# Weights read as every second column of a slab, in the main products of a decoder step

## The chip, the cores and the metric

The kernel runs on one core of one Trainium2 chip. The metric is device time in microseconds of one execution. Before the change it is 1634.39 us (median of three runs, 1634.28 to 1634.63). The profile shows a further execution, instruction by instruction.

## The reference

One step of a decoder layer, for 256 prompt rows and 8 x 4 sample rows with the same weights, so T = 288 rows in all, D_MODEL = 2048 and D_FF = 8192:

```
h = rms_norm(x);  proj = h @ w_in            # 2048 x 10752: conv, attention, memory, gates
y_conv = silu(layer_norm(conv31(glu))) @ w_conv_out
y_sb   = stick_breaking(q, k, v) @ w_sb_out  # 8 heads
y_mem  = softmax_attention(qm, mem) @ w_mem_out   # 4 heads, 256 memory tokens
x = x + (gates * (y_conv, y_sb, y_mem)) summed @ w_o
x = x + square(relu(rms_norm(x) @ w_up)) @ w_down
```

All values are float32. Besides the rows y the new keys, values and convolution rows are returned. Nearly all the arithmetic is in the products of the 288 rows with w_in, w_o, w_up and w_down.

## The kernel before, in words

**Layout.** Activations lie transposed: features on the 128 partitions, the 288 rows along the free side. A product is computed in output tiles of 128 features by 288 rows, one PSUM bank each (pool `pm`). The weight block of 128 x 128 is the operand that TensorE holds (the first operand of `nc.tensor.matmul(ps, w, a)`, line 488), the activation tile of 128 x 288 is the one that it streams, "moving".

**Slabs.** The host lays all weights out in one array `wall` of 504 slabs, each 128 partitions x 1024 floats (`_layout`, from line 1481). From slab 16 on a slab is eight blocks of 128 columns; two slabs make one output tile over 2048 input features. Slabs 0 to 15 belong to the memory keys and values, where `mem_products` (line 541) takes the roles the other way round: 512 slab columns are moving, and the activations are held.

**High and low parts.** To keep float32 accuracy with the faster float32r format, each operand is split: a high part, rounded by a cast, and a low part, the remainder. A weight slab comes by DMA on the sync queue into one of 4 raw tiles `wr` (`load_slab`, line 283), ScalarE casts it into `wh` (line 305), VectorE subtracts into `wl` (line 316). Activations have tiles for `h` and `l` likewise. A block then needs three matmuls: high x high, high x low, low x high. `products` (line 494) lists the 24 matmuls of a slab, first 16 with `wh`, then 8 with `wl`, and gives them to `chunk` (486) six at a time. `conv_products` (550) does the same for the first eight slabs of w_in, in its own order; `main_tile` (509) and `branch_products` (1387) call `products` for everything else. With 488 slabs these are 11,712 matmuls.

**Places in memory.** The `wh` and `wl` tiles are 1088 floats long, and from slab 16 on the weights start `SHIFT` = 5 floats into the tile (`shifted`, line 286). Activation tiles `a` are 320 floats long with the data `AHEAD` = 4 floats in (`Acts`, 325); in the MLP the tiles of the pools `k4` and `s` hold them, 36 floats in (`HOME`, line 1248), three to a tile of 1024 with a distance of 320. For the memory part the activations start 32 floats in, and slabs 0 to 15 at 0.

**Order.** A planner (`Order`, line 75) runs while the program is built. Each piece of work is a generator that asks for an engine and says how long it will take (`MM` = 0.131 us for a matmul of 288 columns) and which flags and buffers it waits for. The planner fixes the order on every engine; on the chip each engine goes through its own list and waits on semaphores. TensorE's list is `main` (1413): memory keys and values, convolution inputs, heads, the three branches with their gates, w_o, then four times 16 tiles of w_up and 16 tiles of w_down. The attention of prompt and samples is mixed in between, up to about 436 us.

Of the kernel before, what the change touches and what calls it, by code (L numbers as in the profile page):

```python
# [14 lines left out]
P = 128  # L15
D_MODEL = 2048
KT = D_MODEL // P
# [19 lines left out]
N_SLABS = 504  # L37
# [37 lines left out]
class Order:  # L75
# [15 lines left out]
    def add(self, gen, rank, at=None):  # L91
        job = Job(gen, rank, self.now.ready if at is None and self.now else at or 0.0)
        self.jobs.append(job)
        was, self.now = self.now, job
        self.step(job)
        self.now = was
# [10 lines left out]
    def give(self, pool, n=1):  # L107
        self.pools[pool] += [self.now.ready] * n
# [57 lines left out]
def pe(us, *flags, **take):  # L166
    return Ask("PE", us, flags, **take)
# [16 lines left out]
def tile_decoder_step(ctx: ExitStack, tc: tile.TileContext, xT, memT, wall, cvec, kmat, ptab,  # L184
# [27 lines left out]
    def bank(p):  # L212
        return tl(p, [P, 512])
# [107 lines left out]
    def start_slab(s):  # L321
        at_slab[:] = [s, order.now.ready]
# [10 lines left out]
    hm, hx = [None] * KT, [None] * KT  # L333
# [149 lines left out]
        done(rm_done)  # L483


    def chunk(ps, todo, first, last):
        for i, (w, a) in enumerate(todo):
            nc.tensor.matmul(ps, w, a, start=(first and i == 0), stop=(last and i == len(todo) - 1))  # L488
# [5 lines left out]
    def products(ps, uses, acts, first=True, last=True, n=T):  # L494

        s = slab_no[0] - 1
        sl = slabs[s]
        high = [(sl.h, c, a, x) for c, a in zip(uses, acts) for x in (0, 1)]
        low = [(sl.l, c, a, 0) for c, a in zip(uses, acts)]
        todo = high + low  # L500
        for i in range(0, len(todo), STEP):
            part = todo[i:i + STEP]
            yield pe(len(part) * MM, *sl.split, *{a.flag for _, _, a, _ in part})
            if i == 0 and first:
                start_slab(s)
            chunk(ps, [(w[:, c:c + P], a.l if x else a.h) for w, c, a, x in part],
                  first and i == 0, last and i + STEP >= len(todo))

    def main_tile(acts, evac, rank=1.0, n_slabs=2):
        yield pe(0.0, pm=1)  # L510
        ps = bank("pm")[:, :T]
        for i in range(n_slabs):
            slab_no[0] += 1
            yield from products(ps, FULL, acts[8 * i:8 * i + 8], i == 0, i == n_slabs - 1)
            give("w")
        add(evac(ps), rank)
# [33 lines left out]
    def conv_products(evacs):  # L550

        s0 = slab_no[0]
        slab_no[0] += KT // 2
        yield pe(0.0, pa=2)
        ps = [bank("pa")[:, :T], bank("pa")[:, :T]]
        lead = 3
        turns = [(k2, o) for k2 in range(lead) for o in (0, 1)] + [(k2, o) for k2 in range(lead) for o in (2, 3)]
        turns += [(k2, o) for k2 in range(lead, KT // 2) for o in range(4)]
        for k2, o in turns:
            s = s0 + k2  # L560
            sl = slabs[s]
            if len(ps) <= o:
                yield pe(0.0, pm=1)
                ps.append(bank("pm")[:, :T])
            todo = []
            for i in range(2):
                w = slice(i * 512 + o * P, i * 512 + (o + 1) * P)
                todo += [(sl.h, w, "h", 2 * k2 + i), (sl.h, w, "l", 2 * k2 + i)]
            for i in range(2):
                todo.append((sl.l, slice(i * 512 + o * P, i * 512 + (o + 1) * P), "h", 2 * k2 + i))  # L570
            yield pe(6 * MM, *sl.split, hx_in[2 * k2], hx_in[2 * k2 + 1])
            if o == 0:
                start_slab(s)
            chunk(ps[o], [(w[:, c], getattr(hx[k], x)) for w, c, x, k in todo], k2 == 0, k2 == KT // 2 - 1)
            if k2 == KT // 2 - 1:
                add(evacs[o](ps[o]), 1.0 + 0.01 * o)
            if o == 3:
                give("w")
        for k in range(KT):
            hx[k].flag = hx_in[k]  # L580
# [806 lines left out]
    def branch_products(br, acts):  # L1387
        for j0 in range(0, KT, 4):
            for j in range(j0, j0 + 4):
                yield from main_tile(hx, gate(br, j))  # L1390
            for j in range(j0, j0 + 4):
                if br == 1:
                    yield from main_tile(acts, branch(br, j), 1.0, 1)
                    continue
                yield pe(0.0, pm=1)
                ps = bank("pm")[:, :T]
                if j % 2 == 0:
                    slab_no[0] += 1
                yield from products(ps, [k * 2 * P + (j % 2) * P for k in range(4)], acts)
                if j % 2:  # L1400
                    give("w")
                add(branch(br, j)(ps), 1.0)
# [10 lines left out]
    def main():  # L1413
        yield from warm_up()
        yield from mem_products()
        yield from conv_products([evac_lin(0, "pa"), evac_gat(0, "pa"), evac_lin(1, "pm"), evac_gat(1, "pm")])
        for j in range(2, CT):
            yield from main_tile(hx, evac_lin(j, "pm"))
# [62 lines left out]
def _layout(inp):  # L1481
    import numpy as np

    a = {k: np.asarray(v) for k, v in inp.items()}
# [8 lines left out]
    x = np.concatenate([a["x_prompt"][0], a["x_sample"].reshape(NS, D_MODEL)], 0)  # L1493

    wall = np.empty((N_SLABS, P, SLAB), np.float32)
    at = [0]

    def put(w, j, r0=0, rows=D_MODEL):
        for half in range(rows // 1024):
            blk = w[r0 + half * 1024:r0 + (half + 1) * 1024, j * P:(j + 1) * P]  # L1500
            wall[at[0]].reshape(P, 8, P)[:] = blk.reshape(8, P, P).transpose(1, 0, 2)
            at[0] += 1
# [40 lines left out]
    for c in range(4):  # L1543
        for f in range(KT):
            put(a["w_up"][0], c * KT + f)
        for j in range(KT):
            put(a["w_down"][0], j, c * D_MODEL)
    assert at[0] == N_SLABS

    cvec = np.zeros((P, NCV), np.float32)  # L1550
    cvec[:, C_GMIX:C_GMIX + KT] = cols(a["g_mix"][0])
# [19 lines left out]
    r, c = i[:, None] % NS, np.arange(NS)[None, :]  # L1571
# [49 lines left out]
```

## Time and profile before

| what | value |
|---|---|
| median of three runs | 1634.39 us |
| span of the profiled execution, first to last instruction | 1632.5 us |
| instructions | 30962 |
| TensorE matmuls busy | 1627.7 us, 100% |
| weight loads (PEld) busy | 1610.3 us, 99% |
| VectorE busy | 992.1 us, 61% |
| ScalarE busy | 739.3 us, 45% |
| GpSimd busy | 139.1 us, 9% |
| DMA | 305.39 MB, mean 187 GB/s |

The times of runs are of a whole execution, the span is from the first instruction to the last within the profiled one; they differ by 1.9 us here. In the profile PE is TensorE's matmuls, PEld its loads of weights, which run under the matmul before them; DVE is VectorE, ACT ScalarE, POOL GpSimd, SP the sync engine with its DMA queue. A row of a group reads: line, engine, operation, tile written <- tiles read, sizes, count, then busy time, mean ns of one and idle time before. Matmuls overlap, so their mean duration is longer than the interval from one start to the next, and a busy share of 100% says only that there was no gap. Clock digits give the granted clock of TensorE in tenths, 9 standing for 90% or more. In the chain in order of time each piece has its start, its length and the number of instructions.

### The profile page before, as it was taken

What the parts mean: (1) busy time and instruction counts of PE and PEld (TensorE: products, weight loads), DVE (VectorE), ACT (ScalarE), POOL (GpSimd) and SP (SyncE); (2) the same over time, 40 slices, a digit from 0 to 9 for tenths busy, and PEclk for the clock granted to TensorE, in tenths of its full rate; (3) what the DMA queues carried; (4) which work ended last, traced back from release to release, by engine and by line L of the source; (5) the groups of instructions that cost most, each with busy time, mean ns of one, the idle gap of its engine ahead of it and who ended that gap; (6) DMA issues with size and microseconds to landing.
All of it is one profiled execution on the core that took longest, in us unless ns stands there. A gap on an engine that the chain in (4) does not pass through costs nothing.

```text
span 1632.5 us, 30962 instructions
## 1 busy us (share of the span) xinstructions
PE 1627.7 (100%) x12786; PEld 1610.3 (99%) x12786; DVE 992.1 (61%) x1471; ACT 739.3 (45%) x1070; POOL 139.1 (9%) x104
## 2 busy tenths in 40 slices
PE   9999999999999999999999999999999999999999
PEld 7999999999999999999999999999999999999999
DVE  8889888877677655565555544455445554455443
ACT  8746766644444534444443333333333333333332
POOL 0020000000000000001222200121001210022100
PEclk9999999999999999999999999999999999999999
DMA  9787465777755555546655555555555555555563
GB/s 339 217 186 251 153 209 189 248 257 252 254 166 169 163 179 167 174 153 212 191 176 168 169 168 168 169 169 174 165 173 170 168 170 169 168 168 168 180 194 99
DMA packets 107103, 305.39 MB, mean 187 GB/s; under 512 B 19922, under 2 KB 29522, under 8 KB 106962
## 3 DMA queue, kind: packets, MB, share of 16 engines
q1 hardware_dynamic: 106818, 303.39, 58.2%
q8 instruction: 100, 1.64, 0.4%
q14 instruction: 41, 0.34, 0.1%
q10 hardware_dynamic: 144, 0.02, 0.0%
HBM read 297.05 MB, written 6.32 MB: 186 GB/s over the span
## 4 chain that ended last, share of the span: by engine, by line
PE 99%; DMA 0%; SPq 0%; ACT 0%; DVE 0%; issue 0%
PE pm L488 93%; PE pm L541 3%; PE pa L488 1%; PE pl L1017 1%; PE pl L1190 0%; PE pa L854 0%; PE pa L855 0%; PE pa L853 0%; DMA wr<-in_wall 0%; PE pl L1033 0%; PE pa L827 0%; PE pa L1144 0%; PE pa L908 0%; PE pa L1141 0%; PE pa L1143 0%; PE pa L1107 0%
## 5 line engine op out<-in xcount | busy, mean ns | idle before, releaser
L305 ACT CAST wh<-wr 128x1024 fp32r<-128x1024 f32 (+1 forms) x520 | 530.3, 1022 | 648.1 <-PE pm L488 597.0
L488 PE MATMUL pm<-a,wh 128*128 128x288 f32 x5184 | 739.1, 293 | 0.0
L316 DVE TENSOR_TENSOR wl<-wr,wh 128x1024 fp32r<-128x1024 f32 (+1 forms) x520 | 617.2, 1190 | 195.2 <-ACT wh L305 190.5
L488 PEld LDWEIGHTS pm<-a,wh 128*128 128x128 f32 x5184 | 696.7, 188 | 1.3 <-issue 1.2
L488 PE MATMUL pm<-a,wl 128*128 128x288 f32 x2592 | 397.0, 292 | 0.0
L488 PEld LDWEIGHTS pm<-a,wl 128*128 128x128 f32 x2592 | 358.4, 188 | 0.0
L488 PE MATMUL pm<-k,wh 128*128 128x288 f32 x2160 | 306.7, 292 | 0.0
L488 PEld LDWEIGHTS pm<-k,wh 128*128 128x128 f32 x2160 | 290.2, 188 | 0.0
L488 PE MATMUL pm<-k,wl 128*128 128x288 f32 x1120 | 171.6, 292 | 0.0
L488 PEld LDWEIGHTS pm<-k,wl 128*128 128x128 f32 x1120 | 155.1, 188 | 0.0
L1346 POOL TENSOR_TENSOR t<-t 128x288 f32<-128x288 f32 x64 | 96.7, 1511 | 599.5 <-DVE t L1343 599.5
L1360 DVE TENSOR_TENSOR a<-a,pm 128x288 f32<-128x288 f32 x64 | 29.0, 454 | 122.4 <-PE pm L488 122.4
L1343 DVE SCALAR_TENSOR_TENSOR t<-pm,rx 128x288 f32<-128x288 f32 x64 | 29.2, 457 | 90.4 <-PE pm L488 90.4
L1349 ACT CAST k<-t 128x288 fp32r<-128x288 f32 x56 | 24.1, 433 | 115.6 <-POOL t L1346 115.6
L1262 DVE TENSOR_TENSOR t<-pm,rx 128x288 f32<-128x288 f32 x48 | 22.0, 458 | 71.5 <-PE pm L488 71.5
L488 PE MATMUL pm<-s,wh 128*128 128x288 f32 x400 | 65.1, 292 | 0.0
L719 DVE SCALAR_TENSOR_TENSOR a<-a,cv,a 128x256 f32<-128x256 f32 x120 | 57.5, 480 | 1.4
L1332 POOL TENSOR_TENSOR t<-t,t 128x288 f32<-128x288 f32 x15 | 21.6, 1441 | 419.3 <-ACT t L1329 419.3
L488 PEld LDWEIGHTS pm<-s,wh 128*128 128x128 f32 x400 | 56.6, 188 | 0.0
L1351 DVE TENSOR_TENSOR k<-t,k 128x288 fp32r<-128x288 f32 x52 | 23.8, 458 | 51.1 <-ACT k L1349 51.1
L541 PE MATMUL pm<-wh,a 128*128 128x512 f32 x128 | 34.6, 391 | 0.2 <-ACT wh L305 0.2
L488 PE MATMUL pm<-s,wl 128*128 128x288 f32 x160 | 33.8, 292 | 0.0
(212 smaller groups left out, 784.4 us busy)
## 6 DMA issues: line engine op xcount, KB each, us to landing
wr<-in_wall SPq DMA_DIRECT2D x488, 512.0 KB, 3.6
wr<-in_wall SPq DMA_DIRECT2D x32, 256.0 KB, 4.8
k<-in_kpool SPq DMA_DIRECT2D x32, 256.0 KB, 5.9
k<-in_vpool SPq DMA_DIRECT2D x32, 256.0 KB, 5.8
k<-in_mkc SPq DMA_DIRECT2D x8, 512.0 KB, 10.2
k<-in_mvc SPq DMA_DIRECT2D x8, 512.0 KB, 6.5
t<-in_xT SPq DMA_DIRECT2D x16, 144.0 KB, 3.7
out_yT<-a SPq DMA_DIRECT2D x16, 144.0 KB, 1.9
```

The source lines that it names most:

```text
L305: nc.scalar.copy(sl.h[:, c], sl.raw[:, c])
L316: nc.vector.tensor_sub(sl.l[:, c], sl.raw[:, c], sl.h[:, c].bitcast(F32))
L488: nc.tensor.matmul(ps, w, a, start=(first and i == 0), stop=(last and i == len(todo) - 1))
L541: nc.tensor.matmul(ps[m], y[:, m * P:(m + 1) * P], z[:, w], start=(k == 0 and j < 2), stop=(k == KT - 1 and j in (4, 5)))
L719: nc.vector.scalar_tensor_tensor(c[:, :NP], up[:, k:k + NP], w, c[:, :NP], op0=ALU.mult, op1=ALU.add)
L1262: nc.vector.tensor_mul(g, ps, rx)
L1332: nc.gpsimd.tensor_add(sq_sum[0], sq_sum[0], res[0])
L1343: nc.vector.scalar_tensor_tensor(r, ps, 0.0, r2, op0=ALU.max, op1=ALU.mult)
L1346: nc.gpsimd.tensor_mul(r, r, r)
L1349: nc.scalar.copy(a.h, r)
L1351: nc.vector.tensor_sub(a.l, r, a.h.bitcast(F32))
L1360: nc.vector.tensor_add(x1[j], x1[j], ps)
```

## The change

In the slabs 16 to 503 the host interleaves each pair of neighbouring 128-column blocks: column c of the first block goes to place 2c of the 256, column c of the second to 2c + 1. A weight operand is then every second float of the 256, from the first or second on. The kernel's `block` makes this view, and both callers of `chunk` use it. The moving operands, the slabs 0 to 15, the casts, the subtractions and the transfers are as they were.

```diff
+    def block(w, c):
+
+        pair = w[:, c // (2 * P) * 2 * P:(c // (2 * P) + 1) * 2 * P]
+        return pair.rearrange("p (c two) -> p two c", two=2)[:, c // P % 2]
...
-            chunk(ps, [(w[:, c:c + P], a.l if x else a.h) for w, c, a, x in part],
+            chunk(ps, [(block(w, c), a.l if x else a.h) for w, c, a, x in part],
...
-            chunk(ps[o], [(w[:, c], getattr(hx[k], x)) for w, c, x, k in todo], k2 == 0, k2 == KT // 2 - 1)
+            chunk(ps[o], [(block(w, c.start), getattr(hx[k], x)) for w, c, x, k in todo], k2 == 0, k2 == KT // 2 - 1)
...
     assert at[0] == N_SLABS
+    for s in range(KT, N_SLABS):
+        v = wall[s].reshape(P, 4, P, 2)
+        v[:] = wall[s].reshape(P, 4, 2, P).transpose(0, 1, 3, 2).copy()
```

## The prediction

> **What bounds the kernel.** I read the page's engine line and its chain first, then the chain in order of time.
>
> ```profile
> PE 1627.7 (100%) x12786; PEld 1610.3 (99%) x12786; DVE 992.1 (61%) x1471; ACT 739.3 (45%) x1070; POOL 139.1 (9%) x104
> ...
> PEclk9999999999999999999999999999999999999999
> ...
> PE 99%; DMA 0%; SPq 0%; ACT 0%; DVE 0%; issue 0%
> ```
>
> ```profile
> 541.70 297.18 PE pm L488 x2286
> ...
> 839.15 790.15 PE pm L488 x6078
> ```
>
> TensorE sets the end, at full granted clock. Line 488 (`chunk`) runs without a break for half the span: 790.15 / 6078 = 130.0 ns from start to start, and 297.18 / 2286 is 130.0 as well. The last columns of the following rows (idle 0.0) say the same. These are all of its groups, and they are the matmuls that the change touches:
>
> ```profile
> L488 PE MATMUL pm<-a,wh 128*128 128x288 f32 x5184 | 739.1, 293 | 0.0
> L488 PE MATMUL pm<-a,wl 128*128 128x288 f32 x2592 | 397.0, 292 | 0.0
> L488 PE MATMUL pm<-k,wh 128*128 128x288 f32 x2160 | 306.7, 292 | 0.0
> L488 PE MATMUL pm<-k,wl 128*128 128x288 f32 x1120 | 171.6, 292 | 0.0
> L488 PE MATMUL pm<-s,wh 128*128 128x288 f32 x400 | 65.1, 292 | 0.0
> L488 PE MATMUL pm<-s,wl 128*128 128x288 f32 x160 | 33.8, 292 | 0.0
> L488 PE MATMUL pa<-a,wh 128*128 128x288 f32 x64 | 11.1, 295 | 0.0
> L488 PE MATMUL pa<-a,wl 128*128 128x288 f32 x32 | 6.8, 292 | 0.0
> ```
>
> Together 11,712. At 130.0 ns they are 1522.6 of the 1632.5 us, so **one nanosecond of the interval is 11.7 us**. The 292 ns of one matmul overlap its neighbours; only the interval counts.
>
> Of what are the 130 ns made? Two other widths, first 512 columns (line 541), then 256 columns (lines 853 to 855), where each matmul also has 128 weight columns of its own:
>
> ```profile
> L541 PE MATMUL pm<-wh,a x77: 389/389/389, 19.7 to 45.5; 128*128 128x512 f32 x77
> L541 PE MATMUL pm<-wl,a x40: 389/389/389, 19.9 to 46.0; 128*128 128x512 f32 x40
> ```
>
> ```profile
> 145.82 0.28 PE L853 MATMUL pa<-a,a 128*128 128x256 f32 x1
> ...
> 146.53 0.30 PE L488 MATMUL pm<-a,wl 128*128 128x288 f32 x1
> ```
>
> 117 starts from 19.7 to 46.0 make 26.3 / 116 = 226.7 ns for 512 columns; six matmuls in 0.71 us make 118.3 ns for 256. So 256 columns more cost 108.4 ns, 0.4234 ns each. Of the 130 ns, 288 columns are 121.9; 8.1 ns are something else. (The two-digit times make the 118.3 uncertain by 1.7, the 121.9 by 2: 120 to 124.)
>
> **What a weight load takes.** It has its own row, PEld, and lies under the matmul before it. Where the moving side is short the load becomes the limit:
>
> ```profile
> 165.69 0.22 PE L853 MATMUL pa<-a,a 128*128 128x128 f32 x1
> 165.75 0.28 PE L854 MATMUL pa<-a,a 128*128 128x128 f32 x1
> 165.86 0.27 PE L855 MATMUL pa<-a,a 128*128 128x128 f32 x1
> 165.97 0.48 PE L488 MATMUL pm<-a,wl 128*128 128x288 f32 x2
> ```
>
> 128 moving columns can follow in 60 ns (165.69 to 165.75, a load already under way), but a sequence settles at 110 (165.75 to 165.97 in two). So 128 neighbouring weight columns load in about 110 ns, 0.86 ns each: half the pace of the moving columns. Of the 130 ns, 20 are slack for the load.
>
> **The change part by part.** *Instructions.* None is added or removed: `block` (a slice and a rearrange while the program is built) makes the same 11,712 weight loads of 128 columns, from every second float of a 256-column stretch. The moving operand, its place, the PSUM side, the casts (line 305), the subtractions (316) and the 512 KB slab transfers stay as they are, since casts and transfers take a slab whole and only its inner order differs. The slabs 0 to 15, read as moving columns by line 541, keep their order. The host's reordering is outside the span. No wait, queue or buffer changes, so each of these costs nothing on its own; the whole question is what a weight load with a step of 8 bytes does to the interval.
>
> *Two streams in one memory.* While a matmul streams 288 columns, the next weights are read for some 110 ns. Now the moving read advances about 110 / 0.4234 = 260 floats in this time, the weight read 128: the former passes the latter at half its speed. If the memory repeats its banks along a row, the two meet at the same bank again and again, and each meeting can hold the stream up. With the step of two the weight read covers 256 floats in the same 110 ns: **both advance at one pace, and keep their distance.** They meet never or always. The code has them far apart: weights start 5 columns into a tile (`SHIFT`), moving columns 4 or 36 (`AHEAD`, `HOME`), in tiles whose lengths are multiples of 64 floats. That the remainder of 8.1 ns is such meetings is inferred. For it speaks that the remainder isn't one number: by 0.4234 ns per column, 512 and 256 columns leave 9.9, and 288 columns, placed by `SHIFT` and `AHEAD`, leave 8.1. (With the 2 ns of uncertainty this is weak evidence.)
>
> No row has a weight read with a step. The bounds of an interval: 120 ns (columns alone, at the low end above), or 2 x 110 = 220 if such a load takes twice as long and becomes the limit. I take 122, the columns alone: nearest to rows that show both streams running, and the load with its 110 still fits under it.
>
> The Trainium skill, "TensorE: Matmul & The Clock Gate", section "Back-to-back issue gap", gives for warm matmuls one column per cycle at 2.4 GHz plus 2.5 ns; worked out for 288 columns that is an estimate of 122.5 ns, and the sum would be 5.9 us less gain than with 122. The trace's 130.0 is above that.
>
> *The sum.* 130.0 - 122.0 = 8.0 ns x 11,712 = 93.7 us (6 to 10 ns: 70 to 117). *What is late next.* Slabs would be wanted every 24 x 122 = 2.93 us instead of 3.12. The suppliers:
>
> ```profile
> SPq L283 <- DVE wl L316: 1153.3, 455, 9.3
> ...
> ACT wh L305 <- PE pm L488: 597.0, 341, 4.1
> ```
>
> ```profile
> wr<-in_wall SPq DMA_DIRECT2D x488, 512.0 KB, 3.6
> ```
>
> ACT's cast waits 597 us for TensorE to give weight tiles back; the slab queue waits for raw tiles, 4 in number, with a landing of 3.6 us against 4 x 2.93. Both have room. VectorE by stretch, and line 488's matmuls in the first one:
>
> ```profile
> 20.00:100.00 80.00, 69.13 (x121) 1.00 0.83 248
> 100.00:150.00 50.00, 47.12 (x82) 1.00 0.85 251
> 150.00:200.00 50.00, 43.89 (x84) 1.00 0.46 142
> 200.00:300.00 100.00, 84.42 (x166) 1.00 0.64 225
> 300.00:400.00 100.00, 74.94 (x141) 1.00 0.69 244
> ```
>
> ```profile
> 20.00:400.00 380.00, 312.24 (x2303) 303.67 (x2304) 1.00 0.70 227
> ```
>
> (The column after the length is VectorE's busy time in the first fence, TensorE's on line 488 in the second.) 2303 matmuls before 400 us would give 18.4 us. Between 100 and 150 us VectorE is 47.12 of 50 busy: the 2.6 us to be gained there (half of some 650 x 8 ns) would bring it to 99%, so I count them lost. Elsewhere before 400 us it would go to 88% or so, in a fixed order with chains through ACT and TensorE; I take a fifth of the other 15.8 as lost, 3 us. After 400 us it is busy for 992.1 less 319.5 and what lies before 20 us (at most 20), some 653 of 1232 us, and nothing is lost. Loss: 5.5 us.
>
> Result: 1632.5 - 93.7 + 5.5 = 1544.3 us of span. The median shown, 1634.39, is 1.9 us above the profiled span; **1546 us**. Its own range: 70 to 117 less 5.5 makes 1523 to 1570.
>
> **Rivals.**
> *Slower: a weight read that touches twice the memory disturbs twice as much.* Place: each load under each matmul of line 488. A load touches 1024 bytes of a partition instead of 512. If the 8.1 ns are paid per stretch of memory fetched and not per meeting, they double: 138.1 ns, + 95 us, 1729 us (with the remainder of 9.9 ns, 1750). It decides as soon as what the doubled fetches add exceeds what the equal pace saves. For it: the remainder exists at all three widths. Against it: by rows with the same 128 weight columns the remainder still differs, 9.9 and 8.1. The Trainium skill, "SBUF — State Buffer", section "Specifications (TRN2)", has lines of 16 bytes, two hits per line needed for full bandwidth, and a penalty at each crossing to a new one: every second fp32 column is just two hits, and crosses twice as often. No run here shows such a read.
>
> *Slower by far: the load itself takes twice as long.* It decides above 130 ns, that is, from a fifth slower than 110. At 220 ns, 90 ns x 11,712 = 1054 us more: 2688. Against it: the moving read takes floats at 0.4234 ns from the same memory, so a path that fetches neighbouring floats at twice the weights' pace exists.
>
> *No change.* The remainder is a fixed price of a matmul, and the load stays hidden: 1634. For it: it is nearly the same, 8 to 10 ns, at all widths. The Trainium skill, "SBUF — State Buffer", section "Who interferes with whom", gives TensorE two independent read ports, for moving columns and for weights, and says that it never waits for anyone. By that the two streams can't meet. The remainder of 8.1 ns neither bears it out nor refutes it. That the change doesn't do what it says (the weights read without a step after all) would end here too.
>
> *Half the gain.* Some meetings stay, as the places were chosen for the old step, and odd blocks start one float later: 126 ns, 46.8 - 3 us, 1591.
>
> **Chances.** Full gain 0.36; half 0.14; no change 0.12; disturbed twice as much 0.30; load as the limit 0.08. A measurement of this kernel tells 0.2% (3.3 us) from no change: faster 0.50, within 0.12, slower 0.38. The likeliest is the full gain, 1546. The range from 1523 to 1750 leaves out the load as the limit and the outer edges of the others, less than 2 in 10.
>
> **What would show it.** Right: the uninterrupted run of line 488 at the end shows 120 to 124 ns per matmul, PEld's records stay at the 188 ns of the row below, and line 541 stays at 226.7. Wrong: 138 ns there (fetches count), 200 or more with PEld starts right behind each other (load as the limit), 130.0 (fixed price). If the interval falls and the span doesn't, VectorE before 400 us is the place to look.
>
> ```profile
> L488 PEld LDWEIGHTS pm<-a,wh 128*128 128x128 f32 x5184 | 696.7, 188 | 1.3 <-issue 1.2
> ```

## The result and the profile after

The changed kernel takes 1672.61 us (median of 4 runs, 1672.35 to 1672.66) against 1634.51 us before (median of 4, the three shown ahead and one more): **2.3% slower**, a ratio of 1.0232 with a 95% interval of 1.0218 to 1.0247. The profiled execution has a span of 1670.9 us, 38.4 us longer than before.

From the page after and its chain in order of time (start, length, number of instructions; line 488 is now 493):

```profile
PE 1666.3 (100%) x12786; PEld 1649.2 (99%) x12786; DVE 992.8 (59%) x1471; ACT 738.5 (44%) x1070; POOL 139.2 (8%) x104
```

```profile
552.42 304.55 PE pm L493 x2286
857.24 810.41 PE pm L493 x6078
```

The number of instructions is the same, and the busy time of VectorE and ScalarE is within 1 us of before. The long run of main products takes 810.41 / 6078 = **133.3 ns per matmul instead of 130.0**; the run before it, 304.55 / 2286, is 133.2. 3.33 ns x 11,712 are 39.0 us, all of the 38.4 and a little more. Nothing else moved: the memory part (line 541, now 546) keeps its interval, 140 starts from 17.7 to 49.3 us in 31.6 / 139 = 227 ns.

```profile
L546 PE MATMUL pm<-wh,a x92: 389/389/389, 18.2 to 48.8; 128*128 128x512 f32 x92
L546 PE MATMUL pm<-wl,a x48: 389/389/397, 17.7 to 49.3; 128*128 128x512 f32 x48
```

One more thing changed, the record of a single weight load: 196 ns in the second to last column, where it was 188.

```profile
L493 PEld LDWEIGHTS pm<-a,wh 128*128 128x128 f32 x5184 | 715.2, 196 | 1.3 <-issue 1.2
```

So the matmuls got slower by a small, even amount, with weight loads under them whose records are 8 ns longer. The questions for the experiments: is it the step of the weights or their place in memory; does the load set the interval; and what is the remainder above the columns' own time, the 8.1 ns that the prediction wanted to remove?

### The profile page after: what moved, and what is told of

It reads as the page before. It is cut to its first block, busy times and chain, and to the rows that moved or that the text cites. A ratio compares the mean times of both kernels' runs of the same rounds, so it can differ in the third digit from the quotient of the medians.

```text
span 1670.9 us, 30962 instructions
## 1 busy us (share of the span) xinstructions
PE 1666.3 (100%) x12786; PEld 1649.2 (99%) x12786; DVE 992.8 (59%) x1471; ACT 738.5 (44%) x1070; POOL 139.2 (8%) x104
## 4 chain that ended last, share of the span: by engine, by line
PE 100%; POOL 0%; DVE 0%; issue 0%; POOLq 0%
PE pm L493 93%; PE pm L546 3%; PE pa L493 1%; PE pl L1022 1%; PE pl L1195 0%; PE pa L859 0%; PE pa L860 0%; PE pa L858 0%; PE pl L1038 0%; PE pa L1414 0%; PE pa L832 0%; PE pa L1149 0%; PE pa L913 0%; PE pa L1146 0%; PE pa L1148 0%; PE pa L640 0%
## 5 line engine op out<-in xcount | busy, mean ns | idle before, releaser
L493 PE MATMUL pm<-a,wh 128*128 128x288 f32 x5184 | 755.6, 297 | 0.0
L493 PEld LDWEIGHTS pm<-a,wh 128*128 128x128 f32 x5184 | 715.2, 196 | 1.3 <-issue 1.2
L493 PE MATMUL pm<-a,wl 128*128 128x288 f32 x2592 | 405.4, 297 | 0.0
L493 PEld LDWEIGHTS pm<-a,wl 128*128 128x128 f32 x2592 | 368.9, 196 | 0.0
L493 PE MATMUL pm<-k,wh 128*128 128x288 f32 x2160 | 313.9, 297 | 0.0
L493 PEld LDWEIGHTS pm<-k,wh 128*128 128x128 f32 x2160 | 298.2, 195 | 0.0
L493 PE MATMUL pm<-k,wl 128*128 128x288 f32 x1120 | 175.3, 296 | 0.0
L493 PEld LDWEIGHTS pm<-k,wl 128*128 128x128 f32 x1120 | 159.6, 196 | 0.0
```

## Experiments

**Single series.** Six kernels are the kernel before with series of matmuls put into `warm_up`, one source line for each form, so that the chain shows each as a piece. The weights come from one tile and the moving columns from another, both filled with ones; both tiles start at the same place modulo 64 floats as the slab tiles do, and moving columns 36 floats in and weights 5 floats in are the places of the main products. (The tiles `a`, with their data 4 floats in, lie 32 floats off by the sizes of the pools between, which makes it the same place modulo 64; this is worked out from the code, no run shows it.) The length of a piece over its count is the mean interval. One line of such a series, with 128 weight columns at a step of 2, 5 floats in:

```diff
+        for i in range(32): nc.tensor.matmul(junk[:, :288], warm[:, 5:260:2], other[:, 36:324], start=True, stop=True)
```

*Places.*

> The kernel before, with a series of matmuls of 288 moving columns put ahead of its own work, 32 for each place of the weights in their tile (25 places, once with neighbouring weight columns and once with every second column; moving columns always 36 floats into their tile). They change nothing that is computed. Theory 'place' (the two reads hold each other up where they fall on the same bank): with neighbouring columns the interval is 130.0 ns at 5 floats and up to 133.3 at others; with every second column it depends strongly on the place, 133 at 5 floats, and at some places at or below 130. Theory 'fetch' (twice the memory costs more wherever it lies): every second column gives 133 to 134 at all places, and neighbouring ones 130 at nearly all.

From its chain, first with neighbouring columns at 3, 5, 8 and 30 floats, then with the step at 2, 5, 40, 44, 48 and 60:

```profile
26.24 4.32 PE pa L1417 x32
...
34.81 4.17 PE pa L1419 x32
...
47.31 4.26 PE pa L1422 x32
...
76.79 4.16 PE pa L1429 x32
...
127.55 4.27 PE pa L1441 x32
...
140.35 4.27 PE pa L1444 x32
...
200.08 4.20 PE pa L1458 x32
204.28 4.27 PE pa L1459 x32
208.55 4.21 PE pa L1460 x32
...
221.26 4.20 PE pa L1463 x32
```

4.16 / 32 is 130.0 ns, 4.26 and 4.27 / 32 are 133.1 and 133.4. Neighbouring columns range from 130 to 135 with the place; 5 floats (L1419) is one of the good places, 8 (L1422) is not. With the step nearly every place pays 133, a few 131 to 132, none 130. So each theory misses a half: "place" its good places with the step, "fetch" the 130 at nearly all places without it. Holding a fixed distance is worth nothing at any of these places; what the step takes away is the good place.

*The load alone, and other steps.*

> The kernel before, with a series of matmuls ahead of its own work, 32 each: 64 and 128 moving columns with weight columns 1, 2, 3, 4 and 8 floats apart, where the load is the limit; 192 to 512 moving columns with steps 1 and 2; 288 columns with steps 3, 4 and 8; 288 columns at 13 places with steps 1 and 2; and every second moving column. If the load itself is slowed by the step, 64 columns show it directly: theory 'fetch' expects 108 ns with step 1, 112 to 116 with step 2 and more with 4 and 8 (up to 215). Theory 'place' expects 108 to 110 with steps 1 and 2, and for 288 columns an interval that changes with the place by 3 ns or more. Over the widths, the part of the interval above 0.4167 ns a column is 10 to 13 ns with either theory.

In this kernel the clock fell during the series with 64 columns (the granted clock is 0.50 from 22 to 80 us, and 1.00 from 86 us on), so the series with 64 and 128 columns were taken again in the next one. At full clock stand, with 288 columns and in order: weights at a step of 3, of 4 and of 8, and weights as neighbours with every second *moving* column:

```profile
132.98 5.56 PE pa L1434 x32
...
160.89 7.47 PE pa L1439 x32
...
198.41 7.72 PE pa L1444 x32
...
347.71 8.21 PE pa L1475 x32
```

The steps of 3, 4 and 8 cost 174, 233 and 241 ns; every second moving column costs 256.6, twice the 130. A step of two is nearly free on the weight side and halves the pace on the moving side. With weights at 5 floats the place of the moving columns counts too: over 13 places in this kernel the interval goes from 130.3 to 135.9 without the step, from 131.2 to 133.4 with it.

> The kernel before with series of matmuls ahead of its own work, which change nothing that is computed: short series of 12 matmuls with 64, 128 and 192 moving columns and weight steps 1 to 4, each after 40 matmuls of 512 columns that keep the clock up (so that the load alone is the limit, at full clock); then 288 moving columns with loads of 128, 112, 96, 80 and 66 weight columns, steps 1, 2 and 4, at two places. Theory 'fetch' (a load's price is the memory lines it opens: 16 bytes each, 32 lines for 128 neighbouring columns, 64 at step 2): the load alone takes 108 ns at step 1, 115 to 120 at step 2, 175 at step 3 and 233 at step 4, and the interval of 288 columns falls with the number of weight columns, with 66 columns at step 2 equal to 128 at step 1 (130). Theory 'fixed' (a price per matmul that the load has no part in): the interval stays at 130 to 133 with 66 columns.

Twelve matmuls each of 64 moving columns, where the load is the limit, for steps 1, 2, 3 and 4, after 40 wide ones each:

```profile
23.25 1.26 PE pa L1415 x12
...
33.93 1.33 PE pa L1417 x12
...
44.42 1.94 PE pa L1419 x12
...
55.53 2.62 PE pa L1421 x12
```

The first of the twelve intervals is short, 0.03 us, as its load was made ahead; the other eleven are (1.26 - 0.03) / 11 = 112 ns, then 118, 174 and 235. So **the load alone is 6% longer at a step of 2, and twice as long at 4.** The Trainium skill, "SBUF — State Buffer", section "Specifications (TRN2)", asks for two hits in each 16-byte line for full bandwidth: on the weight side the runs agree (4 and 2 hits nearly the same, 1 hit twice as long); the moving side, twice as fast, loses half its pace at 2 hits. At 118 the load is under the 130 and doesn't set the interval.

Loads of 66 columns at a step of 2, under 288 moving columns, at 5 and at 28 floats:

```profile
282.89 4.16 PE pa L1465 x32
287.05 4.26 PE pa L1466 x32
```

That is 130.0 and 133.1 ns, inside what "fixed" expected; "fetch" had 130 for such a load, and its fall with the number of columns doesn't show at two places. The next kernel takes 16 places for each form.

*Lines or columns.*

> The kernel before with series of matmuls of 288 moving columns ahead of its own work, each form of load at 16 places (0 to 60 floats by 4): 128, 96, 66 and 34 weight columns at steps 1 and 2, 66 and 34 also at step 4. Lines of 16 bytes opened by a load: 32, 64; 24, 48; 17, 33; 66; 9, 17; 34. Theory 'fetch, at places': the mean over the places grows with the lines, from 130 at 9 lines to 133.3 at 64 and 66, whatever the number of columns; 128 columns at step 1, 66 at step 2 and 34 at step 4 (32 to 34 lines) come out alike, near 131.7. Theory 'columns': it goes by the number of columns, and 66 at step 4 is like 66 at step 1.

Each form has 16 series of 24; the rows are the first series of each form, and the last row is the kernel's own work that follows:

```profile
14.03 3.15 PE pa L1414 x24
...
64.67 3.20 PE pa L1430 x24
...
115.75 3.12 PE pa L1446 x24
...
166.21 3.20 PE pa L1462 x24
...
217.08 3.12 PE pa L1478 x24
...
267.27 3.12 PE pa L1494 x24
...
317.56 3.21 PE pa L1510 x24
...
368.66 3.17 PE pa L1526 x24
...
418.64 3.16 PE pa L1542 x24
...
468.75 3.12 PE pa L1558 x24
...
519.37 2.76 PE pm L543 x12
```

The difference of two starts over 384 matmuls is the mean interval over 16 places:

| weight columns, step | lines of 16 bytes | mean interval, ns |
|---|---|---|
| 34, 1 | 9 | 130.2 |
| 66, 1 | 17 | 130.7 |
| 34, 2 | 17 | 130.5 |
| 96, 1 | 24 | 131.4 |
| 128, 1 | 32 | 131.9 |
| 66, 2 | 33 | 131.0 |
| 34, 4 | 34 | 131.8 |
| 96, 2 | 48 | 132.5 |
| 128, 2 | 64 | 133.0 |
| 66, 4 | 66 | 133.1 |

The mean interval goes by the memory that a load opens, hardly by its columns: 34 columns at step 4 cost what 128 neighbours cost. (66 at step 2 came out 0.7 lower than expected.) Steps 1, 2 and 4 open every line of the stretch that they cover, so lines and length of the stretch can't be told apart here. Single series are less firm than these means: 128 columns at step 2, 16 floats in, gave 133.1 ns in the first kernel and 135.0 in this one. The whole effect is 3 ns. And with a load of 9 lines in place of 32, 130.2 ns are left: **the remainder that the prediction put down to meetings with the weight read stays when most of that read is gone.** A matmul without any load was not run.

*Widths and all places with the step.*

> The kernel before with series of matmuls ahead of its own work: every second weight column at each place from 33 to 63 floats with 288 moving columns; then 256, 320, 384 and 512 moving columns with steps 1 and 2 at eight places each. Theory 'place': some place gives 128 ns or less at step 2, since it holds a fixed distance from the moving read. Theory 'fetch': none falls below 130; most are 133.3, and over the eight places the mean at step 2 is above that at step 1 for every width, by 1 to 7 ns.

No place from 33 to 63 gives less than 131.0, where "place" expected 128 or less at some. For the widths, the rows are the first of eight series each, in the order 256, 320, 384, 512, step 1 and step 2 in turn; L1452 is besides the last place of 256 columns without the step:

```profile
145.03 3.73 PE pa L1445 x32
...
171.62 3.63 PE pa L1452 x32
175.25 3.84 PE pa L1453 x32
...
205.96 4.76 PE pa L1461 x32
...
243.71 4.69 PE pa L1469 x32
...
281.46 5.62 PE pa L1477 x32
...
326.42 5.60 PE pa L1485 x32
...
371.45 7.45 PE pa L1493 x32
...
430.35 7.40 PE pa L1501 x32
...
490.03 43.53 PE pm L543 x192
```

Over 256 matmuls each: 118.0 and 120.0 ns for 256 columns, 230.1 and 233.1 for 512. At 320 and 384 the two steps differ by 0.0 and 0.3 ns, so the second half of the "fetch" expectation, 1 to 7 ns at every width, failed there.

These series also bear on the split of the 130 ns. Their means at step 1 make (230.1 - 118.0) / 256 = 0.438 ns a column, 126 for 288, and leave 4 of the 130; the prediction's two rows, each at one place, made 0.4234 and left 8.1. The place alone moves 256 columns from 113.4 (L1452) to 120.0. How much of an interval is the columns' own is therefore not settled by any run here.

*Pairs of places.*

> The kernel before with series of matmuls of 288 moving columns ahead of its own work, neighbouring weight columns, at 22 places of the moving columns times 6 places of the weights. Looked for: a pair below 130.0. If the 10 ns above the 120 of the columns alone are a price that no place removes, none is more than 1 ns below 130; if they are meetings as well, some pair shows 126.7 or less.

Moving columns at 33 floats with weights at 5, then 36 with 30:

```profile
185.76 3.33 PE pa L1468 x24
...
252.90 3.12 PE pa L1489 x24
```

3.33 / 24 is 139 ns, 3.12 / 24 is 130.0. Of 132 pairs none is below 130.0, so no place tried of either operand takes the remainder away; the worst moving starts are 33, 37 and 61, though 35, odd as well, is among the good ones.

**Whole kernels.**

*The place without the step.* The kernel before, with one number changed:

```diff
-SHIFT = 5
+SHIFT = 8
```

> The kernel before with neighbouring weight columns, only 8 floats into their tiles and not 5. By the series of single places (133.3 ns at 8 floats, 130.1 at 5) the main run's interval goes from 130.0 to 133.3 and the time to 1634 + 39 = 1673, the time of the changed kernel, without any step. If the place matters only within such a series of like matmuls, the time stays at 1634.

1679.60 us, ratio 1.0273 (1.0256 to 1.0290), 6.6 us above what was expected.

```profile
555.82 307.84 PE pm L488 x2286
...
863.92 810.40 PE pm L488 x6078
```

The last run takes 133.3 ns, as after the change, without any step; the run before it takes 134.7, and that it pays more there is not explained. A place alone can cost what the change cost.

*Every second slab.*

```diff
-    def block(w, c):
+    def block(w, c, s):
+        if s % 2 == 0:
+            return w[:, c:c + P]
...
-    for s in range(KT, N_SLABS):
+    for s in range(KT + 1, N_SLABS, 2):
```

> The change for odd slabs only: in even slabs the weights stay neighbouring columns. If each matmul pays for its own load, half of the 38 us: 1653 to 1655, with intervals of 130.0 and 133.3 slab by slab. If the loss comes from alternating between starts of even and odd blocks, or from anything that spreads, nearer to 1634 or 1672.

1655.97 us, ratio 1.0128 (1.0111 to 1.0145), in the last run 801.16 / 6078 = 131.8 ns. That is 20.8 us, a little over half. In the timeline slabs of 24 matmuls alternate, 3.13 and 3.20 us, 130.4 and 133.3 ns a matmul: each matmul pays for its own load.

```profile
849.78 801.16 PE pm L495 x6078
```

```profile
1201.57 2.25 PE L495 MATMUL pm<-k,wh 128*128 128x288 f32 x16
...
1204.70 1.63 PE L495 MATMUL pm<-k,wh 128*128 128x288 f32 x11
...
1207.90 2.24 PE L495 MATMUL pm<-k,wh 128*128 128x288 f32 x16
```

*The step at another place.* The changed kernel with `SHIFT = 40`, then 60:

> The changed kernel with the weights 40 instead of 5 floats into their tiles. In the single series the step of two gave 131.4 and 131.2 ns at 40 and 41 floats (133.3 at 5 and 6). If that holds in the kernel: 1634.5 + 1.3 x 11.7 = 1650, against 1672.6 with 5. If the place no longer matters with the step in a mixed series: 1672.

> As before, with 60 floats, where the single series gave 131.1 at 60 and 61 floats: 1647 to 1649 if that holds, 1672 if not. Neither theory expects a time below the kernel before.

1648.46 us, ratio 1.0080 (1.0063 to 1.0097), and 1648.45, ratio 1.0079 (1.0063 to 1.0096). The long run at the end is the same to the last digit in both; this is the one with 60:

```profile
846.62 796.91 PE pm L493 x6078
```

796.91 / 6078 = 131.1 ns, as the series at 60 floats had (131.2). Nearly two thirds of the loss, 24.2 of 38.1 us, come back by choosing the place anew, and the last 1.1 ns don't. No version tried is faster than the kernel before.

## Why the prediction was wrong

*What bounds the kernel, and the price of a nanosecond.* Right: TensorE sets the end, only the 11,712 matmuls changed, and 3.33 ns at 11.7 us each account for the 38.4 us. Casts, transfers and waits cost nothing, as worked out.

*The load.* Right that it stays covered: 112 ns alone and, at a step of 2, 118, under 130. It isn't unchanged, though: the records, expected to stay at 188 ns, went to 196. The rival "the load itself takes twice as long" is what happens at a step of 4 (235 ns), not of 2.

*Two streams in one memory.* **This is the step that failed.** It read the 8.1 ns above the columns' own time as meetings of the moving read with the weight read, and took them all off: 122 ns, where 133.3 were measured. A load of 34 columns, 9 lines in place of 32, still leaves 130.2 ns on the mean over places, and with the step no place went below 131. The lowest series of 288 columns, whatever its load, is 128.8 (3.09 / 24, with 34 columns at a step of 2). So at most a small part of the remainder was due to the weight read, and an equal pace had nothing there to save. What the weight read does add lies on top, from nothing to 5 ns by place, and the kernel before was at a place where it adds next to nothing.

The evidence that the prediction gave for this step was weak, as it said itself, and weaker than it thought: of its three remainders, 9.9, 9.9 and 8.1, the two equal ones are equal by construction, since the pace of 0.4234 was drawn through these two rows. The third differs by less than its uncertainty of 2 ns. And the pace belongs to the places of the two rows, as the widths above show.

*The rival "twice the memory disturbs twice as much".* Right in its direction: over places, the interval grows with the lines that a load opens, from 131.9 to 133.0 for twice as many. Wrong in what it doubled: the 8.1 ns hardly depend on the load, and it gave 1729 us against 1672.6 measured. Of the 3.33 ns, 1.9 are the good place lost (131.9 over places less 130.0), 1.1 the lines, and the last 0.3 is that 5 floats is a little worse than the mean with the step. The kernels with 40 and 60 floats agree with this split: 1.1 ns are what they don't get back.

*The range.* 1523 to 1750 holds the 1672.6, but only because it spans theories that point opposite ways. None of them had 133 ns.

*No change, by independent read ports.* The Trainium skill, "SBUF — State Buffer", section "Who interferes with whom", has TensorE's two read ports wait for no one. The table above speaks against it: one engine's weight reads move the interval of its own moving stream by 3 ns.

*VectorE before 400 us.* Never tested, as nothing became faster.

What stays open: why the interval depends on the places of the two operands, and on which of their bits; whether the lines of a load or the length of its stretch count for the interval; why the steps are of about 1.1 and 3.3 ns; and what a matmul with a small load spends beyond its columns, and how much that is.

## What to carry to other kernels

Before a remainder is put down to an interaction, take one partner away: series with a load of 34 columns instead of 128 would have shown that the remainder was not its doing. And a price per column drawn through two rows needs a third row, at the same places, before what is left over can be read. Weights at a step of 8 bytes cost little where the load is covered (118 against 112 ns alone), moving columns at that step cost half the pace, and weights at 16 bytes make the load the limit. In a kernel whose matmuls run without a gap, operand places were worth up to 2.7% here, and any change of the access pattern asks for a new search of them, with series of single forms: their intervals held in the whole kernels, but for one stretch (134.7 ns at 8 floats, where the series had 133.1).

## What the runs showed that was not expected

The place of the weights within 64 floats moves the interval by up to 5 ns of 130 (130.0 to 135.0), that of the moving columns by more (139 at 33 floats). The load of 128 neighbouring weight columns can be shortened to 34 without any gain in the interval of 288 columns beyond 1.7 ns.

The load alone, where it is the limit, takes 1.8 ns for each line of 16 bytes once lines are what holds it up: 118 / 64 at a step of 2, 174 / 96 at 3, 235 / 128 at 4. Neighbouring columns, 112 / 32 = 3.5 ns a line, are paced otherwise. A step of 8 opens as many lines as 4 over twice the memory and costs nearly the same, 241 against 233 ns. TensorE's clock has no part in the price of a line: at a granted clock of 0.50 a load with a step of 4 took 7.45 / 32 = 233 ns (second kernel of series, 64 moving columns), while one with a step of 3 went from 174 to 6.83 / 32 = 213. That a step of 2 comes out just above the 112 ns of neighbours, and no more, follows from these two paces.
